# Differential attention: the second softmax's scores leave PSUM by ScalarE, the first softmax's sum moves into the head norm's constant, and three heads share one norm chain

## The chip, the core and the metric

The kernel runs on one core of a Trainium2 chip. The core has a matrix engine (TensorE, PE in the profile; its weight loads are listed apart as PEld), a vector engine (VectorE, DVE), a scalar engine for activations and copies (ScalarE, ACT), a general engine (GpSimd, POOL), and SyncE (SP), which issues most of the DMAs. PE reads SBUF and writes PSUM; DVE and ACT read and write both. Each engine runs its own queue in order, and semaphores tie the queues together. The metric is the device time of one execution in microseconds (us), lower is better; the median of several runs is compared.

## What is computed

One block of a hybrid network over 1024 tokens of width 1024, with 256 tokens of context: a Hyena branch, a differential attention branch, a gated mix of both, and a gated FFN. The change lies in the attention alone. It has 4 heads; each has two softmaxes over 1024+256 keys with 64-wide queries and keys, and one value of 128. Cut to what matters:

```python
def block(qi):                                   # 128 queries of a head
    s = einsum('bhiqd,bhikd->bhiqk', qi, k) * HEAD_DIM ** -0.5     # i = 0, 1
    p = softmax(s, axis=-1)
    a = p[:, :, 0] - lam * p[:, :, 1]
    return einsum('bhqk,bhkv->bhqv', a, v)

def rmsnorm(x, g):
    return x * rsqrt(mean(x * x, axis=-1) + EPS) * g

def heads_out(o, subln_g, lam_init):
    return rmsnorm(o, subln_g) * (1.0 - lam_init)
```

Everything is fp32. A product that needs full precision is made of three matmuls on numbers split into a high and a low half (`hi`, `lo`).

## The kernel before

The program is written as tiles with names; a scheduler orders each engine's queue by its own estimate of when operands and buffers come free, in the main following the order of the code. A tile with a tag shares a ring of buffers with its like, and an allocation waits for the oldest user of the ring.

The attention stage loops over 4 heads (`hd`) and, in each, over 4 groups of 256 queries (`qg`): 16 calls of `attn_group`. `load_head` brings the keys `KS` (one tile for each softmax) and the values `VH`, `VL` from DRAM, and each group loads its queries `Q`. For each of the two blocks of 128 queries (`qt`) and each softmax `i`, PE writes the scores in chunks of 512, 512 and 256 keys into a PSUM bank `S` (tag `S`, 3 banks). Line 808, on DVE, takes each chunk out of PSUM into `pr` (tag `P`, `NP` = 5 buffers of 1280), multiplies it by -1/8 and keeps a running minimum, `prev`, from chunk to chunk. `act(pr, pr, AF.Exp, ...)` then runs on ACT over all 1280 and adds up the softmax's sum into a column of `st_`. DVE takes the reciprocals of both sums (L813) and multiplies the second by `neglam`; ACT scales the second exponentials by it (`AF.Copy` with `scale`); and a `scalar_tensor_tensor` on DVE (helper `stt`, L80) makes the first exponentials times their reciprocal plus the scaled second ones. Calls go through helpers, so rows of the profile often carry the helper's line: `tt` is L77, `stt` L80, `ts` L83, `act` L86.

Then `mid` runs, a list of other work that the group may have in its middle, and the weighted sum follows: PE transposes the probabilities into `pt` (L826), ACT copies them to `ah` (L830) and DVE makes the low half `al` (L77), and PE adds up 30 matmuls into `pv` (L835 to L837). ACT copies `pv` to `ov` and squares it into `osq`, PE sums the squares over partitions (L844) and DVE copies the sums into two columns of `ssall` (L847).

While heads 0 to 2 run, PE fills in with the projections of the next head (`qkv_parts`; L134, operands `h_hi`, `h_lo`). In head 3 it fills in with `hy_up` (L134, operand `z`), the first product of the mix, and with the head norms `y_norm(0)` to `y_norm(2)`. `FILL3` sets which: its entries 10, 11, 12 are `y_norm`, the others `hy_up`. The first entry is `(10, 0)`, `y_norm(0)` and then `hy_up(0)`. Both take a PSUM tile of tag `accb`, two buffers, in the order of the code. `open_mix` frees the projections' operands and loads `z`.

A norm starts with `y_rstd`: 13 small steps on DVE from 8 columns of `ssall` to `rs`, by a bit trick and three Newton steps (`rsqrt_tail`). `y_scale` multiplies the identity by four columns of `rs` on DVE (`dg`, L83), PE broadcasts them by a matmul with ones (L893), and an `stt` scales `yr`. Head 3's own norm follows the loop: `y_rstd(NH - 1, cp)`, then `y_scale` on a PSUM tile `bcp`.

## Time and profile before

| | |
|---|---|
| median of 3 runs | 1852.08 us (1849.85 to 1852.66) |
| profiled execution, its own time | 1849.88 us |
| its span, first to last instruction | 1847.7 us |
| PE busy | 1751.7 us, 95% of the span |
| DVE busy | 1278.9 us, 69% |
| ACT busy | 751.5 us, 41% |
| POOL busy | 58.1 us, 3% |
| TensorE clock granted, mean | 0.979 |
| attention stage (first scores to the last head's sums) | about 632 to 945 us of the span |

The profile lists for each group of instructions its line, its engine, what it writes and reads, its busy time and the idle time of the engine just before it with the instruction that ended it. Matmuls overlap in their pipeline, so that a matmul's duration is longer than the distance to the next; a gap between weight loads tells more of a waiting PE than a gap between matmuls. Shares over the whole span mix stages with different limits, and the questions here are put to the attention stage alone.

### The profile page before, as it was taken

What the parts mean: (1) busy time and instruction counts of PE and PEld (TensorE: products, weight loads), DVE (VectorE), ACT (ScalarE), POOL (GpSimd) and SP (SyncE); (2) the same over time, 40 slices, a digit from 0 to 9 for tenths busy, and PEclk for the clock granted to TensorE, in tenths of its full rate; (3) what the DMA queues carried; (4) which work ended last, traced back from release to release, by engine and by line L of the source; (5) the groups of instructions that cost most, each with busy time, mean ns of one, the idle gap of its engine ahead of it and who ended that gap; (6) DMA issues with size and microseconds to landing.
All of it is one profiled execution on the core that took longest, in us unless ns stands there. A gap on an engine that the chain in (4) does not pass through costs nothing.

```text
span 1847.7 us, 22554 instructions
## 1 busy us (share of the span) xinstructions
PE 1751.7 (95%) x8122; PEld 1408.0 (76%) x8122; DVE 1278.9 (69%) x2277; ACT 751.5 (41%) x1179; POOL 58.1 (3%) x63
## 2 busy tenths in 40 slices
PE   7999989999996999999998899989999999899997
PEld 3588778787875888887876687777778888788886
DVE  5888787776868689898849547967886666323234
ACT  3511323222232466767755257634344343222221
POOL 0000000000000212110100000000000000000000
PEclk9899999999998999999999899989999999999998
DMA  8344533324266834437348743333354225967432
GB/s 331 99 171 175 176 120 131 107 93 154 80 236 230 242 92 137 126 115 233 110 160 285 249 145 119 126 114 114 137 175 156 103 103 178 318 216 210 137 92 68
DMA packets 190111, 293.92 MB, mean 159 GB/s; under 512 B 15235, under 2 KB 110223, under 8 KB 188720
## 3 DMA queue, kind: packets, MB, share of 16 engines
q1 hardware_dynamic: 183776, 284.82, 46.6%
q10 hardware_dynamic: 6224, 7.66, 1.4%
q8 instruction: 64, 1.05, 0.2%
q14 instruction: 47, 0.39, 0.1%
HBM read 213.78 MB, written 78.64 MB: 158 GB/s over the span
## 4 chain that ended last, share of the span: by engine, by line
PE 72%; DVE 18%; DMA 5%; issue 2%; ACT 2%; ACTq 0%; SPq 0%; DVEq 0%
PE pj L1181 20%; PE ps L1043 17%; PE ps L134 16%; DVE pair L77 4%; PE S L804 4%; DVE quad L77 3%; PE pt L826 2%; PE psf L392 2%; PE psf L393 2%; PE psf L537 1%; PE pv L835 1%; PE psf L576 1%; PE psf L378 1%; PE pv L837 1%; DVE wlo L77 1%
## 5 line engine op out<-in xcount | busy, mean ns | idle before, releaser
L77 DVE TENSOR_TENSOR wlo<-wraw,whi 128x1024 fp32r<-128x1024 f32 (+1 forms) x192 | 181.4, 948 | 262.9 <-ACT whi L126 128.5
L126 ACT CAST whi<-wraw 128x1024 fp32r<-128x1024 f32 (+1 forms) x119 | 118.1, 993 | 206.6 <-PE ps L1043 159.0
L134 PE MATMUL ps<-h_hi,wlo 128*128 128x512 f32 x640 | 174.3, 402 | 0.7 <-DVE wlo L77 0.7
L134 PE MATMUL ps<-h_hi,whi 128*128 128x512 f32 x640 | 172.5, 400 | 0.0
L134 PE MATMUL ps<-h_lo,whi 128*128 128x512 f32 x640 | 168.0, 395 | 0.0
L134 PEld LDWEIGHTS ps<-h_hi,wlo 128*128 128x128 f32 x640 | 119.6, 190 | 25.2 <-DVE wlo L77 1.6
L134 PEld LDWEIGHTS ps<-h_lo,whi 128*128 128x128 f32 x640 | 120.0, 189 | 24.4
L134 PEld LDWEIGHTS ps<-h_hi,whi 128*128 128x128 f32 x640 | 119.2, 190 | 22.9
L1181 PE MATMUL pj<-hfc,whi 128*128 128x512 f32 x528 | 131.1, 390 | 0.0
L1181 PEld LDWEIGHTS pj<-hfc,whi 128*128 128x128 f32 x528 | 99.1, 188 | 21.1
L804 PE MATMUL S<-KS,Q 128*128 128x512 f32 (+1 forms) x384 | 107.6, 374 | 3.1 <-DVE pr L808 2.6
L486 ACT COPY gt<-ps 128x512 f32<-128x512 f32 x56 | 32.9, 588 | 188.5 <-PE ps L134 149.0
L1181 PE MATMUL pj<-hfb,whi 128*128 128x512 f32 x352 | 91.7, 404 | 8.7 <-ACT whi L1173 8.6
L1181 PE MATMUL pj<-hfa,whi 128*128 128x512 f32 x352 | 88.9, 393 | 1.4 <-ACT whi L1173 1.3
L1181 PEld LDWEIGHTS pj<-hfb,whi 128*128 128x128 f32 x352 | 67.0, 192 | 27.0 <-ACT whi L1173 11.2
L1173 ACT CAST whi<-s 128x512 fp32r<-128x512 f32 x66 | 40.5, 620 | 100.9 <-DVE s L77 81.8
L1181 PEld LDWEIGHTS pj<-hfa,whi 128*128 128x128 f32 x352 | 65.6, 188 | 16.4 <-ACT whi L1173 2.2
L804 PEld LDWEIGHTS S<-KS,Q 128*128 128x128 f32 x384 | 64.4, 189 | 17.4 <-DVE pr L808 9.4
L1173 ACT CAST whi<-wraw 128x512 fp32r<-128x512 f32 x88 | 53.3, 619 | 56.6 <-PE pj L1181 46.8
L1181 PE MATMUL pj<-hfc,wlo 128*128 128x512 f32 x264 | 70.5, 389 | 0.0
L77 DVE TENSOR_TENSOR quad<-psf,xb 128x512 f32<-128x512 f32 x64 | 41.0, 683 | 35.9 <-ACT xb L250 35.9
L77 DVE TENSOR_TENSOR al<-pt,ah 128x512 fp32r<-128x512 f32 x80 | 52.2, 685 | 10.9 <-ACT ah L830 10.2
(492 smaller groups left out, 3618.2 us busy)
## 6 DMA issues: line engine op xcount, KB each, us to landing
wraw<-win SPq DMA_DIRECT2D x46, 512.0 KB, 3.7
wraw<-wdown SPq DMA_DIRECT2D x88, 256.0 KB, 3.3
wada_t<-wada SPq DMA_DIRECT2D x32, 512.0 KB, 7.5
wraw<-wgate SPq DMA_DIRECT2D x28, 512.0 KB, 3.3
wraw<-wupf SPq DMA_DIRECT2D x28, 512.0 KB, 3.7
ad<-kp SPq DMA_DIRECT2D x44, 256.0 KB, 2.1
w_ada<-wada SPq DMA_DIRECT2D x16, 512.0 KB, 6.6
kspec<-quad SPq DMA_DIRECT2D x8, 1024.0 KB, 3.9
```

What stands on the lines that cost most here:

```text
L77: (eng or V).tensor_tensor(out=out, in0=a, in1=b, op=op)
L126: A.copy(out=hi, in_=raw)
L134: T.matmul(out=ps, lhsT=w[:, k * P:(k + 1) * P], rhs=xs[k][j], start=start and i == 0, stop=stop and i == len(seq) - 1)
L378: T.matmul(out=ps, lhsT=a[:, cs], rhs=b, start=i == 0, stop=i == 2)
L392: T.matmul(out=out, lhsT=mfm(part, r), rhs=gen[r][:, 0:256], start=True, stop=False)
L393: T.matmul(out=out, lhsT=mfm(pb, rb), rhs=gen[rb][:, 256:512], start=False, stop=True)
L486: A.copy(out=gt, in_=ps)
L804: T.matmul(out=S[:, :cn], lhsT=Q[j][:, i, qt * P:(qt + 1) * P], rhs=KS[i][:, c0:c0 + cn], start=j == 0, stop=j == 1)
L826: T.transpose(out=pt[:, b * 256 + qt * P:b * 256 + (qt + 1) * P], in_=av[qt][:, kt * P:(kt + 1) * P], identity=ident)
L1043: T.matmul(out=acc[b].rearrange("p (m c) -> p m c", m=4), lhsT=xs[kk][i == 1][:, b * P:(b + 1) * P], rhs=w[i == 2][kk], start=first and (k ...
L1173: A.copy(out=hi, in_=src)
L1181: T.matmul(out=ps, lhsT=w[a][:, k * P:(k + 1) * P], rhs=xs[k][b], start=i == 0, stop=i == 11)
```

## The change

Four things change, all in the attention stage.

1. The probabilities are no longer divided by the first softmax's sum s0. The exponentials are combined as P0 + (-lam s0 / s1) P1, which is s0 times what it was. The head norm that follows is made of sums of squares, so that a factor s0 cancels if its constant EPS is multiplied by s0 squared. The sums s0 are kept in a new tile `s0all`, one column for each 128 queries. ACT's scaling pass over the second exponentials goes away.
2. The second softmax's three score chunks leave PSUM by `A.copy` on ACT; one DVE instruction over all 1280 elements, in place in SBUF, then multiplies by -1/8 and finds the minimum. The first softmax's chunks stay as they were.
3. `y_rstd` is called once for heads 0 to 2, inside `y_norm(0)`, on 24 columns, with two more steps (the square of `s0all`, and its product with EPS), and once for head 3.
4. `y_scale` makes `dg` on ACT.

```diff
+    s0all = ap.tile([P, 32], F32, name="s0all")
...
             st_ = a2.tile([P, 12], F32, tag="st", bufs=4, name="st_")
+            c0_ = hd * 8 + qg * 2 + qt
+            sums = [s0all[:, c0_:c0_ + 1], st_[:, 3:4]]
...
+                    if i == 1:
+                        A.copy(out=pr[:, c0:c0 + cn], in_=S[:, :cn])
+                        continue
 
                     mc = st_[:, 6 + 3 * i + c:7 + 3 * i + c]
                     V.tensor_scalar(out=pr[:, c0:c0 + cn], in0=S[:, :cn], scalar1=-0.125, scalar2=prev,
                                     op0=ALU.mult, op1=ALU.min, accum_out=mc)
                     prev = mc
-                act(pr, pr, AF.Exp, bias=prev, scale=-1.0, accum_out=st_[:, 2 + i:3 + i])
+                if i == 1:
+                    prev = st_[:, 9:10]
+                    V.tensor_scalar(out=pr, in0=pr, scalar1=-0.125, scalar2=None, op0=ALU.mult, op1=ALU.min,
+                                    accum_out=prev)
+                act(pr, pr, AF.Exp, bias=prev, scale=-1.0, accum_out=sums[i])
                 pp.append(pr)
-            V.reciprocal(out=st_[:, 4:6], in_=st_[:, 2:4])
-            tt(st_[:, 5:6], st_[:, 5:6], neglam, ALU.mult)
-            act(pp[1], pp[1], AF.Copy, scale=st_[:, 5:6])
-            stt(pp[0], pp[0], st_[:, 4:5], pp[1], ALU.mult, ALU.add)
+
+            V.reciprocal(out=st_[:, 4:5], in_=sums[1])
+            stt(st_[:, 5:6], sums[0], neglam, st_[:, 4:5], ALU.mult, ALU.mult)
+            stt(pp[0], pp[1], st_[:, 5:6], pp[0], ALU.mult, ALU.add)
...
-    def y_rstd(hd, pool_):
-        cs = slice(hd * 8, hd * 8 + 8)
-        w = pool_.tile([P, 24], F32, tag="yrs", bufs=2, name="yrs")
-        ts(w[:, 0:8], ssall[:, cs], 1.0 / P, EPS, ALU.mult, ALU.add)
-        rsqrt_tail(w[:, 8:16], w[:, 0:8], w[:, 16:24])
-        ts(rs[:, cs], w[:, 8:16], 1.0 - LAM_INIT, None, ALU.mult, ALU.bypass)
+    def y_rstd(h0, h1, pool_):
+
+        cs, n = slice(h0 * 8, h1 * 8), (h1 - h0) * 8
+        w = pool_.tile([P, 72], F32, tag="yrs", bufs=1, name="yrs")
+        m, r, q = [w[:, i * 24:i * 24 + n] for i in range(3)]
+        tt(r, s0all[:, cs], s0all[:, cs], ALU.mult)
+        ts(m, ssall[:, cs], 1.0 / P, None, ALU.mult, ALU.bypass)
+        stt(m, r, EPS, m, ALU.mult, ALU.add)
+        rsqrt_tail(r, m, q)
+        ts(rs[:, cs], r, 1.0 - LAM_INIT, None, ALU.mult, ALU.bypass)
...
-            ts(dg[:, b * P:(b + 1) * P], ident, rs[:, c0:c0 + 1], None, ALU.mult, ALU.bypass)
+            act(dg[:, b * P:(b + 1) * P], ident, AF.Copy, scale=rs[:, c0:c0 + 1])
...
     def y_norm(hd):
-        y_rstd(hd, a2)
+        if hd == 0:
+            y_rstd(0, NH - 1, a2)
...
-    y_rstd(NH - 1, cp)
+    y_rstd(NH - 1, NH, cp)
```

The scheduler puts the stage's queues into another order with this. Three places follow; the line numbers of the changed kernel are some 3 to 14 higher than those of the old one (L808 is L814 there, L826 is L836, L893 is L907; L810 is the new copy on ACT, L819 the new pass on DVE).

DVE in the second head, one block of 128 queries, before: six chunks leave PSUM, with `al` of the group before between them, and the two tiny steps and the `stt` follow.

```order
L808 TENSOR_SCALAR pr,st__6063<-S,st__6063 128x256
L808 TENSOR_SCALAR pr,st__6096<-S 128x512
L808 TENSOR_SCALAR pr,st__6096<-S,st__6096 128x512
L813 RECIPROCAL st__6063<-st__6063 128x2
L808 TENSOR_SCALAR pr,st__6096<-S,st__6096 128x256
L77 TENSOR_TENSOR al<-pt,ah 128x512 x2
L77 TENSOR_TENSOR st__6063<-st__6063,lamc 128x1
L808 TENSOR_SCALAR pr,st__6096<-S 128x512
L80 SCALAR_TENSOR_TENSOR pr<-pr,st__6063 128x1280
```

The same place now:

```order
L819 TENSOR_SCALAR pr,st__6064<-pr 128x1280
L814 TENSOR_SCALAR pr,st__6097<-S 128x512
L814 TENSOR_SCALAR pr,st__6097<-S,st__6097 128x512
L814 TENSOR_SCALAR pr,st__6097<-S,st__6097 128x256
L824 RECIPROCAL st__6064<-st__6064 128x1
L80 SCALAR_TENSOR_TENSOR st__6064<-s0all,lamc,st__6064 128x1
L80 SCALAR_TENSOR_TENSOR pr<-pr,st__6064 128x1280
L814 TENSOR_SCALAR pr,st__6230<-S 128x512
L819 TENSOR_SCALAR pr,st__6097<-pr 128x1280
```

Three chunks of each pair are replaced by one pass over `pr`, which stands between chunks of other blocks.

ACT in the first head, third group, before: exponentials (two names of `st_` each) and scalings (`pr<-pr,st`), with `ah` between them.

```order
L86 ACTIVATE pr,st__4982<-pr,st__4982 128x1280
L86 ACTIVATE pr,st__5187<-pr,st__5187 128x1280
L86 ACTIVATE pr<-pr,st__4982 128x1280
L86 ACTIVATE pr,st__5187<-pr,st__5187 128x1280
L830 CAST ah<-pt 128x512 x2
L86 ACTIVATE pr<-pr,st__5187 128x1280
```

The same place now:

```order
L810 COPY pr<-S 128x512
L840 CAST ah<-pt 128x512 x2
L86 ACTIVATE pr,s0all<-pr,st__5188 128x1280
L810 COPY pr<-S 128x256
L840 CAST ah<-pt 128x512 x2
L86 ACTIVATE pr,st__5188<-pr,st__5188 128x1280
L86 ACTIVATE pr,s0all<-pr,st__5221 128x1280
```

The scalings are gone, and copies out of `S` stand behind exponentials and `ah` on the same queue.

PE where the first `hy_up` matmul stands (operand `z`), before: in the weighted sum of a group, soon after the projections of the heads have run out.

```order
L837 MATMUL pv<-al,VH 128x256
L826 MATMUL pt<-ident,pr 128x128 x8
L804 MATMUL S<-KS,Q 128x256 x2
L134 MATMUL ps<-z_7114,whi 128x512
L835 MATMUL pv<-ah,VH 128x256
L836 MATMUL pv<-ah,VL 128x256
L134 MATMUL ps<-z_7115,whi 128x512
```

The same place now, where `ps<-dg,ones` are the broadcasts of `y_norm(0)`:

```order
L807 MATMUL S<-KS,Q 128x256 x2
L807 MATMUL S<-KS,Q 128x512 x4
L907 MATMUL ps<-dg,ones 128x512
L836 MATMUL pt<-ident,pr 128x128 x2
L807 MATMUL S<-KS,Q 128x256
L907 MATMUL ps<-dg,ones 128x512
L134 MATMUL ps<-z_7115,whi 128x512
L134 MATMUL ps<-z_7116,whi 128x512
```

`hy_up` now follows the second broadcast directly and runs in a row. Between the last projection matmul and the first `hy_up` matmul stand 136 matmuls before and 213 now.

## Rows read from the trace of the kernel before

**Rows 1.** The page's busy times: engine, busy us, share of the span, instructions.

```profile
PE 1751.7 (95%) x8122; PEld 1408.0 (76%) x8122; DVE 1278.9 (69%) x2277; ACT 751.5 (41%) x1179; POOL 58.1 (3%) x63
```

**Rows 2.** Windows: us; PE, PEld, DVE, ACT, POOL busy (instructions); clock, DMA share, GB/s.

```profile
632.00:945.00 313.00, 307.42 (x1772) 253.81 (x1772) 272.80 (x705) 213.54 (x325) 39.66 (x23) 1.00 0.41 132
842.00:867.00 25.00, 23.10 (x132) 16.83 (x131) 23.18 (x68) 17.81 (x28) 0.82 (x1) 1.00 0.89 303
867.00:945.00 78.00, 77.83 (x453) 64.47 (x454) 62.67 (x160) 53.99 (x89) 6.54 (x4) 1.00 0.32 104
```

**Rows 3.** Waits of weight loads, 632 to 945 us: total us, times, longest.

```profile
PEld S L804 <- DVE pr L808: 9.4, 22, 1.3
PEld pv L835 <- ACT ah L830: 8.5, 27, 1.0
PEld pv L844 <- ACT osq L86: 3.9, 12, 0.4
PEld pt L826 <- DVE pr L80: 3.1, 5, 1.2
PEld pv L837 <- DVE al L77: 3.1, 11, 0.6
```

**Rows 4.** Waits of PE's weight loads, 842 to 867 us.

```profile
PEld S L804 <- DVE pr L808: 3.5, 9, 0.8
...
PEld pt L826 <- DVE pr L80: 1.2, 1, 1.2
...
PEld pv L837 <- DVE al L77: 0.9, 2, 0.6
```

**Rows 5.** Timeline, 856 to 862 us: start, us, engine, instruction, idle before.

```profile
856.19 4.55 PE L804 MATMUL S<-KS,Q 128*128 128x256 f32 x14
...
861.70 0.63 PEld L826 LDWEIGHTS pt<-ident,pr 128*128 128x128 f32 x6 [1.17 <-DVE pr L80]
```

**Rows 6.** Timeline, 635 to 644 us: evictions and `stt` on DVE, weight loads.

```profile
635.31 0.69 DVE L808 TENSOR_SCALAR_CACHE_REDUCE pr<-S 128x512 f32<-128x512 f32 x1
...
635.92 0.48 DVE L808 TENSOR_SCALAR_CACHE_REDUCE pr<-S,st__4477 128x256 f32<-128x256 f32 x1
...
636.33 0.75 DVE L808 TENSOR_SCALAR_CACHE_REDUCE pr<-S,st__4477 128x512 f32<-128x512 f32 x1
...
637.00 0.08 DVE L808 DVE_READ_ACCUMULATOR pr<-S,st__4477 128x1 f32 x1
...
643.64 1.58 PEld L134 LDWEIGHTS ps<-h_hi,whi 128*128 128x128 f32 x7
643.68 1.54 DVE L80 SCALAR_TENSOR_TENSOR pr<-pr,st__4477 128x1280 f32<-128x1280 f32 x1
```

**Rows 7.** Lines by form, whole span: busy us, mean ns of one, idle before.

```profile
L753 ACT CAST c_hi<-cx 128x256 fp32r<-128x256 f32 x8 | 2.8, 406 | 11.3 <-DVE cx L83 11.3
...
L83 DVE TENSOR_SCALAR sy<-sy 128x512 f32<-128x512 f32 x6 | 2.6, 426 | 0.2
```

**Rows 8.** Timeline, ACT: a scaling pass, copies out of PSUM.

```profile
642.14 1.37 ACT L86 ACTIVATE pr<-pr,st__4477 128x1280 f32<-128x1280 f32 x1 [0.20 <-DVE st__4477 L77]
...
697.25 0.37 ACT L839 COPY ov<-pv 128x256 f32<-128x256 f32 x1 [1.41 <-PE pv L837]
...
706.19 1.04 ACT L830 CAST ah<-pt 128x512 fp32r<-128x512 f32 x2
```

**Rows 9.** Timeline, 945 to 950 us, the last head's norm.

```profile
945.67 0.17 DVE L83 TENSOR_SCALAR yrs<-ssall 128x8 f32<-128x8 f32 x1
...
948.38 1.66 DVE L83 TENSOR_SCALAR dg<-ident,rs 128x128 f32<-128x128 f32 x8
949.33 0.30 PEld L893 LDWEIGHTS bcp<-dg,ones 128*128 128x128 f32 x2 [1.99 <-ACT whi L126]
```

**Rows 10.** Timeline, 705 us, POOL and DVE side by side.

```profile
705.00 2.40 POOL L77 TENSOR_TENSOR wlo<-wraw,whi 128x1024 fp32r<-128x1024 f32 x1 [26.30 <-ACT whi L126]
...
705.33 2.62 DVE L77 TENSOR_TENSOR t<-t,sw 128x512 f32<-128x512 f32 x1
```

## The prediction

> **What bounds the kernel now.** I read the page's busy times first, then the stage by windows, then who waits for whom on PE. Over the whole span PE is busy 1751.7 us (95%) and DVE 1278.9 [rows 1]. The change touches the attention stage, from the first score matmul at 632 us to the last head's sums at 945. There DVE is busy 272.80 of 313.00 us (87%), ACT 213.54 (68%), and PE counts as busy for 307.42, while its weight loads fill 253.81 [rows 2]. A busy PE hides gaps, since the modelled ends of matmuls overlap, so I go by the waits of the weight loads: 9.4 us (22 times) for DVE to take a score bank out of PSUM, 3.1 us (5 times) for the combined probabilities, 3.1 us (11 times) for the low half `al`; against ACT 8.5 us (27 times) for `ah` and 3.9 us (12 times) for the squares [rows 3]. That is 28 us, about 15.6 of them DVE's. Some 0.04 us of each is the ordinary gap between two loads (seven of 0.19 in 1.58 us, rows 6), so perhaps 25 us of the 313 can be won at the very most. The granted clock is 1.00 in each of these windows [rows 2], so it is no part of the sum.
>
> The loss is uneven. From 842 to 867 us the weight loads fill 16.83 of 25 us (67%), from 867 to 945 64.47 of 78 (83%) [rows 2], and 5.6 of DVE's 15.6 us fall into those 25 us [rows 4]. There PE has no projection to fill in with. Seven pairs of score matmuls are spread over 4.55 us, and then the transposes wait 1.17 us for the `stt` on DVE [rows 5]. I call it the bare stretch.
>
> **Evictions.** For each 128 queries the second softmax now loses three DVE instructions that read PSUM. Counted from start to start, since neighbours overlap, they take 0.61, 0.41 and 0.67 us [rows 6], 1.69 together, with the accumulator reads inside. It gains one DVE pass over 128x1280 in SBUF with the same minimum, which the trace does not show. From above: the `stt` over 1280 takes 1.54 with the overlap [rows 6], so about 1.45 without. From below: the same 512 elements take 0.426 us from SBUF in a plain multiply and add, against 0.69 from PSUM with the minimum [rows 6, 7], and the slope of rows 6, 0.26 us for 256 elements, gives 0.61+0.78=1.39 at the slow rate and about 0.87 at the fast one. I take 1.39, as the row of the same operation is the nearest, and keep 0.87 to 1.45. Times 32: 9.6 us of DVE work less (7.7 to 26).
>
> The Trainium skill, in "VectorE: DVE Perf Modes", section "The perf-mode tier table", gives a plain fp32 `tensor_scalar` in SBUF twice the rate of one that reads PSUM; by it the pass would cost about 0.8 us, an estimate from its 1227 ns for 2048 elements. The plain multiply of rows 7 agrees with that; no row shows a pass that also keeps a minimum.
>
> ACT gains three copies out of PSUM, by the rows of like size 1.04 for the two wide ones and 0.37 for the 256 wide, and loses the scaling of 1280 elements, 1.37 [rows 8]: 1.41 against 1.37, so nothing. The path from the last score bank to the finished probabilities keeps its length too. Before: a DVE eviction, an exponential, two tiny steps, the ACT scaling, the `stt`. After: an ACT copy, the DVE pass, an exponential, two tiny steps, the `stt`. The reciprocal and the step after it stay two tiny DVE steps.
>
> **Norms.** Three chains of 13 DVE steps become one of 15. A chain alone runs from 945.67 to 948.38, 0.208 a step [rows 9], so 24 steps are 5.0 us. The 24 `dg` steps of heads 0 to 2 leave DVE at 0.207 each (eight in 1.66, rows 9): 5.0 us. On ACT they cost less than the 0.41 of a 256-wide instruction [rows 7], so under 10 us, in a stage in which ACT is idle for 99. The last head's chain is two steps longer (0.4 us), and its eight `dg` stand on ACT too; they lie before a broadcast for which PE already waits 1.99 us [rows 9], so I give this 0, at most +1.
>
> **DVE's sum**: 9.6+5.0+5.0 = 19.6 us of 272.8, which leaves 253 (81%). One thing can eat into it: an addition of two SBUF tiles over 512 elements took 2.62 us while POOL ran 2.40 beside it [rows 10]. The new pass reads SBUF, its forerunners PSUM. POOL is busy 13% of the stage [rows 2]; if the pass suffers the same way, 32 x 0.13 x about 1 us gives 4 us back. I leave that in the range.
>
> **What of it reaches the end.** Outside the bare stretch, PE waits for DVE's evictions 9.4-3.5=5.9 us, for the `stt` 1.9 and for `al` 2.2 [rows 3, 4]; less 0.04 us for each of the 26, 9 us. DVE's idle time grows from 40 to 60 us, so its busy-to-idle ratio falls from 6.8 to 4.2, and I let the waits fall in that proportion (0.62). Of the score banks only half still wait for DVE. So 5.5 x (1-0.31) = 3.8 us go on the scores and 3.5 x 0.38 = 1.3 on the others: -5.1. Against it, scores now wait for ACT, behind exponentials as long as the scaling pass, 1.37 us, on its queue [rows 8]; `ah`, five to a group and 80 in all, costs PE 8.5 us [rows 3], and the 96 new ones have three banks of slack, so +0.5 (0 to +3). With the norms' work out of head 3, -1.5 (0 to -3). The waits for `ah` and for the squares I leave as they are, since ACT's load hardly changes.
>
> The bare stretch grows. In the order before, 136 matmuls lie between the last projection of the heads and the first `hy_up` matmul, now 213: `y_norm(0)` stands ahead of `hy_up(0)` and takes its PSUM tile first, and its constant now needs head 2's sums. The stretch loses (0.83-0.67) x 25 = 4 us now; at 213/136 it would lose 6.3, and 6% less DVE work takes a little off. So +2 (0 to +8; the upper end is three times today's loss, as if DVE alone set the pace there).
>
> On SP the loads of `Q` and of weights change places by a few issues; no PE wait of the stage ends on a DMA [rows 3], so 0. Sum: -5.1+0.5-1.5+2 = -4.1, with ends at -13 and +8. The profiled execution took 1849.88 us (span 1847.7), so 1845.8; the median of the three runs lies 2.2 higher, at 1852.08, so **1848.0** on that scale. The FFN behind it is shifted unchanged.
>
> **Rivals.** *The relief goes deeper* (0.14): the SBUF pass runs at the fast rate, 32 x 0.52 = 16.6 us more off DVE. At the rate of the sum above, 5.1 us for 19.6, that is 4 to 5 more: 1843. For it speaks the plain multiply of rows 7, against it that this one has a minimum to keep. By the rule of the Trainium skill cited above it would come out like this.
> *The relief stays in DVE's idle time* (0.31): DVE is in order, and the new pass waits for the third ACT copy, itself queued behind exponentials; the waits change their name but not their length. 1850 to 1854, no difference that can be seen. For it speaks that the path keeps its length, and that this also happens if the pass costs 1.45 plus POOL's share, when DVE sheds too little.
> *The merged norm starves PE* (0.23), the slower side: `hy_up` is held behind a constant that needs three heads, and the longer stretch runs at DVE's pace. From +6 in the stretch on it outweighs the gains elsewhere: +8 with -4 there, 1856. For it: the 213 matmuls and the 67% of rows 2. Against it: the projections that are not used there fill PE later and are not lost.
>
> **Chances and range.** The forecast itself, 2 to 8 us faster than the median, 0.32. A measurement of this kernel can tell about 0.2%, 3.7 us. Faster by more than that: most of the forecast and the deeper case, 0.45; within: 0.31; slower: 0.24. The range 1837 to 1858 leaves out the ends of both tails; the forecast's own range is 1844 to 1850.
>
> **What would show it.** Right: DVE busy near 253 us in the stage, ACT within 8 of 214, weight loads waiting for evictions under 6 us in total, PE's bare stretch longer but not emptier. A pass over 1280 near 0.8 us means the deeper case. Wrong: a total of PE waits as large as before with ACT's name on the score banks, or over 8 us of waits between the last projection and the first `hy_up` matmul.

## The result, and the profile after

The changed kernel is slower: 1864.62 us median (1862.02 to 1870.7, 6 runs) against 1852.37 for the kernel before, measured beside it (1849.85 to 1854.43, 6 runs). The ratio of the runs is 1.0077, with a 95% interval of 1.0065 to 1.0089; the two medians alone give 1.0066. The prediction was 1848.0 and its range ended at 1858. The profiled span grew from 1847.7 to 1862.4 us.

The attention stage now runs from 632 to 965 us of the span. Its busy times (us; PE, PEld, DVE, ACT, POOL with instructions; clock, DMA share, GB/s), to be read against [rows 2]:

```profile
632.00:965.00 333.00, 317.49 (x1775) 253.88 (x1774) 257.82 (x530) 222.91 (x413) 40.84 (x22) 0.99 0.40 124
```

DVE did shed the work: 272.8 us became 257.8, in a stage that is 20 us longer. But the waits of the weight loads did not shrink with it. They answer to [rows 3]; the columns are the total in us, how often, and the longest:

```profile
PEld pv L845 <- ACT ah L840: 13.4, 42, 0.8
PEld pv L847 <- DVE al L77: 9.4, 19, 2.1
PEld S L807 <- DVE pr L814: 9.1, 22, 1.2
PEld pt L836 <- issue: 6.0, 11, 3.0
PEld pt L836 <- DVE pr L80: 5.8, 9, 1.0
PEld S L807 <- ACT pr L810: 3.7, 12, 0.8
PEld pv L854 <- ACT osq L86: 2.0, 6, 0.6
```

The waits for `ah` grew from 8.5 to 13.4 us, for `al` from 3.1 to 9.4, for the combined probabilities from 3.1 to 5.8. DVE's score banks are half as many and still cost 9.1 us. The 3.0 us put down to "issue" are a weight load just ahead of a matmul that itself waits for the `stt`, as a timeline below shows.

**Where the time went.** For each matmul I took the distance to the next one, less the lower quartile for its form, as lost time, and added it up in three parts: from the first scores to the last projection matmul, from there to the first product of the mix (the bare stretch), and on to the last head's sums.

| | to the last projection | bare stretch (its length) | to the stage's end | stage | behind it to the last matmul |
|---|---|---|---|---|---|
| before | 13.4 | 6.8 (26.7 us) | 6.0 | 313.8 us | 74.9 lost in 898.1 |
| after | 24.1 | 16.2 (48.1 us) | 3.7 | 333.2 us | 69.8 lost in 893.3 |

So the stage is 19.4 us longer: 10.7 are lost among the projections, 9.4 in the bare stretch, 2.3 come back behind it, and 1.6 this measure doesn't place. The stages that follow give another 4.8 us back. Two losses have to be explained, each about 10 us.

### The profile page after: what moved, and what is told of

It reads as the page before. It is cut to its first block, busy times and chain, and to the rows that moved or that the text cites. A ratio compares the mean times of both kernels' runs of the same rounds, so it can differ in the third digit from the quotient of the medians.

```text
span 1862.4 us, 22438 instructions
## 1 busy us (share of the span) xinstructions
PE 1755.4 (94%) x8122; PEld 1404.6 (75%) x8122; DVE 1262.6 (68%) x2095; ACT 762.8 (41%) x1275; POOL 59.8 (3%) x63
## 3 DMA queue, kind: packets, MB, share of 16 engines
q8 instruction: 64, 1.05, 0.2%
## 4 chain that ended last, share of the span: by engine, by line
PE 65%; DVE 19%; DMA 7%; ACT 4%; issue 3%; SPq 0%; POOL 0%; ACTq 0%; DVEq 0%
PE pj L1196 19%; PE ps L1058 16%; PE ps L134 13%; DVE pair L77 4%; DVE quad L77 3%; PE S L807 3%; PE psf L392 2%; PE psf L393 2%; PE pt L836 1%; PE psf L537 1%; DVE pr L80 1%; PE psf L576 1%; PE psf L378 1%; PE pv L845 1%; DVE wlo L77 1%
## 5 line engine op out<-in xcount | busy, mean ns | idle before, releaser
L134 PEld LDWEIGHTS ps<-h_lo,whi 128*128 128x128 f32 x640 | 119.9, 189 | 24.3
L807 PEld LDWEIGHTS S<-KS,Q 128*128 128x128 f32 x384 | 63.5, 193 | 19.9 <-DVE pr L814 9.1
```

The source lines that it names most:

```text
L134: T.matmul(out=ps, lhsT=w[:, k * P:(k + 1) * P], rhs=xs[k][j], start=start and i == 0, stop=stop and i == len(seq) - 1)
L807: T.matmul(out=S[:, :cn], lhsT=Q[j][:, i, qt * P:(qt + 1) * P], rhs=KS[i][:, c0:c0 + cn], start=j == 0, stop=j == 1)
```

## The experiments

Twenty kernels are compared below; each was timed against the kernel before on its own chip, so the ratio counts and not the median. An interval is some 0.001 to 0.0025 to either side. The columns on the right are read from one profiled execution of each kernel: the loss as above, when its first scores start, how long the stage is from there to the last head's sums, and how long it is from these to the last matmul.

| kernel | ratio (95%) | lost to the last projection | lost in the bare stretch (its length) | first scores at | stage | behind it |
|---|---|---|---|---|---|---|
| before | 1 | 13.4 | 6.8 (26.7) | 631.6 | 313.8 | 898.1 |
| changed kernel | 1.0077 (1.0065 to 1.0089) | 24.1 | 16.2 (48.1) | 631.6 | 333.2 | 893.3 |
| e1: changed, a chain per head | 1.0085 (1.0059 to 1.0110) | 24.3 | 11.2 (30.7) | 634.6 | 329.4 | 892.0 |
| e2: before + merged chain | 1.0047 (1.0030 to 1.0064) | 11.3 | 16.9 (51.5) | 632.6 | 323.5 | 895.9 |
| e3: before + ACT evictions and pass | 1.0105 (1.0087 to 1.0124) | 19.8 | 11.5 (32.4) | 635.8 | 329.5 | 899.3 |
| e4: before + s0 in the constant | 1.0040 (1.0027 to 1.0052) | 17.8 | 13.5 (30.9) | 633.7 | 325.6 | 895.8 |
| e5: changed, `hy_up(0)` first | 1.0063 (1.0048 to 1.0078) | 24.0 | 1.0 (5.4) | 631.2 | 330.2 | 891.8 |
| e6: changed, DVE evictions | 0.9990 (0.9974 to 1.0006) | 16.0 | 17.0 (45.1) | 636.6 | 322.0 | 889.4 |
| e7: e6 with a chain per head | 1.0008 (0.9992 to 1.0024) | 18.3 | 12.2 (33.2) | 628.8 | 323.6 | 891.3 |
| e8: changed, six buffers | 1.0090 (1.0072 to 1.0109) | 25.6 | 18.5 (51.5) | 632.6 | 337.4 | 889.2 |
| e9: before + `dg` on ACT | 1.0016 (1.0003 to 1.0030) | 14.6 | 9.1 (28.6) | 635.4 | 318.4 | 895.7 |
| e10: changed, no DVE pass | 1.0036 (1.0018 to 1.0055) | 17.8 | 14.5 (46.8) | 633.2 | 322.3 | 895.9 |
| e11: before + two more DVE passes | 1.0028 (1.0012 to 1.0044) | 13.4 | 7.8 (27.8) | 635.7 | 318.2 | 900.7 |
| e14: changed, exponentials from PSUM | 1.0019 (1.0006 to 1.0032) | 23.2 | 12.8 (35.4) | 632.9 | 325.6 | 890.8 |
| f1: changed, POOL's work on DVE | 1.0029 (1.0016 to 1.0042) | 18.9 | 21.2 (41.6) | 624.7 | 332.3 | 892.3 |
| f3: e14, POOL's work on DVE | 0.9988 (0.9979 to 0.9998) | 17.4 | 13.9 (37.3) | 627.8 | 321.1 | 894.2 |
| f4: e6, POOL's work on DVE | 0.9987 (0.9974 to 0.9999) | 14.6 | 16.1 (49.2) | 626.0 | 320.9 | 897.9 |
| f5: before, POOL's work on DVE | 0.9995 (0.9984 to 1.0006) | 15.3 | 8.4 (24.3) | 625.7 | 320.5 | 897.6 |
| g1: f4 with a chain per head | 0.9949 (0.9929 to 0.9969) | 15.0 | 6.5 (28.9) | 626.6 | 315.0 | 897.0 |
| g2: f3 with a chain per head | 0.9978 (0.9962 to 0.9993) | 15.3 | 10.9 (29.5) | 632.6 | 317.9 | 892.1 |

How far can one execution be trusted? The kernel before and e11 have the same order on every engine up to 870 us. Their first scores start 4.1 us apart, and from there to 857 us that distance stays within 0.1 us. So a stretch of the stage repeats well, but the time ahead of it does not: the fourteen kernels with the same 2621 matmuls in the same order ahead of the first scores reach them at 628.8 to 636.6 us. Some of these executions (e3, e6, e11) are also 4 to 5 us above the median of their kernel. So I compare stages to the microsecond, and what lies ahead and behind only roughly.

### The merged chain and the evictions, one at a time (e1, e2, e3, e5)

e1, a chain per head in the changed kernel:

```diff
-        if hd == 0:
-            y_rstd(0, NH - 1, a2)
+        y_rstd(hd, hd + 1, a2)
```

> The changed kernel with one change taken back: each head's norm chain runs alone on its 8 columns, as before, so that y_norm(0) needs head 0 alone. The order then has 127 matmuls between the last projection and the first hy_up matmul, not 213. Theory N (the merged chain holds hy_up back and starves PE): the changed kernel loses about 16 us of PE's time between 850 and 890 us where the old one loses about 6, so 8 to 10 of its 12 us come back: 1853 to 1856. Theory E (the evictions on ACT are the cause, through a longer ping-pong of ACT and DVE in every group): the stretch matters little, 1861 to 1864.

e2, the merged chain alone on the kernel before:

```diff
-        y_rstd(hd, a2)
+        if hd == 0:
+            y_rstd(0, NH - 1, a2)
```

> The kernel before with one change alone: the norm chain of heads 0 to 2 in one call inside y_norm(0). Evictions, scaling and dg stay on their engines. The order has 235 matmuls in the bare stretch, before 136. Theory N: slower than before by 6 to 12 us, 1858 to 1864, and all of it between the last projection and the first hy_up matmul. Theory E: within 3 us of before, or a little faster, since DVE loses 26 small steps.

e3, the evictions alone on the kernel before (ACT's scaling pass stays):

```diff
+                    if i == 1:
+                        A.copy(out=pr[:, c0:c0 + cn], in_=S[:, :cn])
+                        continue
...
+                if i == 1:
+                    prev = st_[:, 9:10]
+                    V.tensor_scalar(out=pr, in0=pr, scalar1=-0.125, scalar2=None, op0=ALU.mult, op1=ALU.min,
+                                    accum_out=prev)
```

> The kernel before with one change alone: the second softmax's chunks leave PSUM by ACT and one DVE pass finds the minimum; the scaling on ACT stays, so ACT gains three copies per 128 queries. The bare stretch in the order is 138 matmuls, as before (136). Theory N: within 4 us of before. Theory E: slower by 5 to 12 us, with PE waiting for al, ah and the transposes in the projections' part, 632 to 840 us.

e5, the changed kernel with `hy_up(0)` ahead of `y_norm(0)`, so that products of the mix may run before the constant is there:

```diff
-FILL3 = ((10, 0), (1, 11), (2, 12), (3, 4, 5))
+FILL3 = ((0, 10), (1, 11), (2, 12), (3, 4, 5))
```

> The changed kernel with one entry of FILL3 turned round: hy_up(0) ahead of y_norm(0), so that the fill-in product takes its PSUM tile first. The bare stretch in the order falls to 36 matmuls. Theory N: the loss of 16 us between 850 and 890 shrinks to what the landing of z leaves, 4 to 8 us, so 1852 to 1857. Theory E: 1860 to 1864.

Alone, the merging costs 0.47%, and its loss lies in the bare stretch, which doubles (26.7 to 51.5 us) and loses 16.9 us instead of 6.8, while the projections' part is no worse than before. The evictions alone cost 1.05%, as much as the whole change or more, in both parts. But the prices don't add up: without the merging the changed kernel is not measurably faster (1.0085, with 0.0025 to either side; its stage is 3.8 us shorter), and with `hy_up` first it gets back 0.14%, which the intervals leave open: the stretch shrinks to 5.4 us, but the 16 us that it lost are lost behind it instead (20.1 us from there to the stage's end).

### What the relief of DVE is worth (e4, e6, e7, e9)

e4 takes the changed kernel's `s0all` and `y_rstd`, with DVE's evictions, a chain per head and `dg` on DVE. e9 is the kernel before with one line of the change:

```diff
-            ts(dg[:, b * P:(b + 1) * P], ident, rs[:, c0:c0 + 1], None, ALU.mult, ALU.bypass)
+            act(dg[:, b * P:(b + 1) * P], ident, AF.Copy, scale=rs[:, c0:c0 + 1])
```

e6 is the changed kernel without the evictions on ACT:

```diff
-                    if i == 1:
-                        A.copy(out=pr[:, c0:c0 + cn], in_=S[:, :cn])
-                        continue
...
-                if i == 1:
-                    prev = st_[:, 9:10]
-                    V.tensor_scalar(out=pr, in0=pr, scalar1=-0.125, scalar2=None, op0=ALU.mult, op1=ALU.min,
-                                    accum_out=prev)
```

and e7 is e6 with e1's edit on top.

> Before, with the first sum moved into the norm's constant alone: the scaling pass on ACT goes (32 x 1.37 us), the evictions stay on DVE, dg stays on DVE, one chain per head. Theory E (what costs is the second softmax leaving PSUM by ACT, with the minimum in a pass behind it): nothing of the loss is here; the path from the last score bank to the probabilities is 1.4 us shorter, so 0 to 8 us faster than before, ratio 0.996 to 1.000. Theory O (any edit of this block puts the projections in lumps, and the lumps cost): projections' part 5 or more us slower, ratio 1.003 or more. Theory N (the merged chain alone costs): like E.

> The changed kernel with the second softmax's scores taken out by DVE again (tensor_scalar with the running minimum, three to a bank row), the rest as changed: s0 in the constant, merged chain, dg on ACT. Theory E: the projections' part (632 to 832) goes back to the loss of before, 1.3 to 2 us in 20; the stretch behind the projections still loses about 9 us more than before by the merged chain; the tail gives 4 to 5 back: ratio 0.998 to 1.004. Theory N: everything stays as in the changed kernel, 1.006 to 1.009. Theory O: projections' part still about 9 us slower, 1.005 or more.

> The changed kernel without ACT evictions and without the merged chain: s0 in the constant and dg on ACT remain. Theory E: neither loss is here, so ratio 0.993 to 0.999 (faster by 2 to 12 us, of which 4 to 5 in the stages behind the attention, if they go with dg on ACT). Theory O: 1.003 or more, lost in the projections' part. Against e6 it gives the price of the merging when the evictions are DVE's: about 9 us if the prices are additive, as they were not in e1.

> Before, with the dg steps alone on ACT (0.40 us each, eight to a head). If the 4.7 us that the changed kernel gets back behind the last head's sums belong to dg on ACT: the stretch from the last sums to the end is 897 to 899 us instead of 902, ratio 0.996 to 0.999. If they belong to the other edits: 902 us, ratio 0.999 to 1.001. Theory O: stage longer by 5 us or more.

The comparison of e6 with the changed kernel is the largest in the set: 0.9990 against 1.0077, for the evictions alone; the stage is 11.2 us shorter, and the loss among the projections falls from 24.1 to 16.0 us. That is Theory E, that the evictions on ACT, with the pass behind them, are what costs. Its second half fell: e4 takes 38 us of the stage's work off ACT and is 0.4% slower, with a stage 11.8 us longer; e9 takes 4 us off DVE, puts 7 on ACT, and is no faster. Theory O asked for a ratio like e4's (1.003 or more), while e6 and e7 went against it.

e7 missed as well. Theory E gave it 0.993 to 0.999 and it came to 1.0008, so that against e6 the merging costs nothing even where DVE evicts. From e4 to e7 little changes but that `dg` goes to ACT (`yrs` also has one buffer instead of two): that is worth 0.32%, while on the kernel before the same step costs 0.16%. So an edit's price hangs on the order that the scheduler makes of all of them, and a difference of 0.3% does not by itself show the mechanism that an edit was made for. Each of the four edits alone lengthens the stage of the kernel before, the merging by 9.7 us, the evictions by 15.7, the first sum by 11.8 and `dg` by 4.6: 42 us, where all four together cost 19.4. No run tunes the order anew for the changed kernel, so how much of a price belongs to an edit and how much to its order stays open.

The 4.8 us that the stages behind the attention give back are not `dg`'s either: with it alone 2.4 us of them show (895.7 us behind the last sums, against 898.1), and e11, whose edit lies in the stage, differs by as much the other way (900.7). What they belong to stays open.

### Buffers, the pass, and the bare stretch's edge (e8, e10, e11, e14)

e8 sets `NP = 6`. e10 drops the pass; the second exponential runs without a maximum:

```diff
-                if i == 1:
-                    prev = st_[:, 9:10]
-                    V.tensor_scalar(out=pr, in0=pr, scalar1=-0.125, ...)
-                act(pr, pr, AF.Exp, bias=prev, scale=-1.0, accum_out=sums[i])
+                if i == 1:
+                    act(pr, pr, AF.Exp, scale=0.125, accum_out=sums[i])
+                else:
+                    act(pr, pr, AF.Exp, bias=prev, scale=-1.0, accum_out=sums[i])
```

e14 has ACT take the exponentials straight out of the banks, without copies:

```diff
                     if i == 1:
-                        A.copy(out=pr[:, c0:c0 + cn], in_=S[:, :cn])
+                        act(pr[:, c0:c0 + cn], S[:, :cn], AF.Exp, scale=0.125, accum_out=st_[:, 9 + c:10 + c])
                         continue
...
                 if i == 1:
-                    prev = st_[:, 9:10]
-                    V.tensor_scalar(out=pr, in0=pr, scalar1=-0.125, ...)
-                act(pr, pr, AF.Exp, bias=prev, scale=-1.0, accum_out=sums[i])
+                    tt(st_[:, 9:10], st_[:, 9:10], st_[:, 10:11], ALU.add)
+                    tt(sums[1], st_[:, 9:10], st_[:, 11:12], ALU.add)
+                else:
+                    act(pr, pr, AF.Exp, bias=prev, scale=-1.0, accum_out=sums[i])
```

e11 is the kernel before with a delay that was meant for the bare stretch:

```diff
+            if hd == NH - 1 and qg == 0 and qt == 1:
+                for _ in range(2):
+                    ts(pp[0], pp[0], 1.0, None, ALU.mult, ALU.bypass)
             stt(pp[0], pp[0], st_[:, 4:5], pp[1], ALU.mult, ALU.add)
```

> The changed kernel with six buffers of probabilities instead of five. Ring theory (a second softmax's tile is now taken at its first copy and held through copies, pass, exponential and combination, so that the ring of five runs out and the next scores have nowhere to go): the loss of the projections' part falls from about 24 us to 16 or less, ratio 1.000 to 1.004. Hop theory (the chain from the last score bank over copy, pass, exponential to the combination is what is late, and more buffers don't shorten it): ratio 1.006 to 1.009 as in the changed kernel.

> The changed kernel without the pass over 1280 elements on DVE: the second softmax's scores leave by ACT as changed, and its exponential runs with scale 1/8 and no maximum taken off (that part of the computation is left out). Hop theory: with the pass both the hop to DVE and 45 us of DVE work are gone, the combination is no longer late, the projections' part loses 16 us or less, ratio 0.990 to 0.999. Bank theory (the loss is in score banks that wait for ACT behind 1.4 us exponentials): the waits of weight loads for ACT's copies remain or grow beyond 4 us and the ratio stays above 1.003.

> The kernel before with two more passes of DVE over 1280 elements (times one) ahead of the combination of head 3's first group, in the stretch without projections; nothing else is changed. Edge theory (the stretch of before runs just above where the granted clock falls, and any longer wait there drops it): granted clock 0.5 for 6 us or more after that wait, and the stretch longer by more than the added DVE time allows, 5 to 7 us in all: ratio 1.0025 to 1.004. Without an edge: clock 1.00, and at most the two passes' own 2 x 1.4 us or less: ratio 0.9995 to 1.0015.

> The changed kernel with the second softmax's exponentials taken by ACT directly out of the three score banks, scale 1/8, no maximum taken off (that part is left out), their three sums added in two tiny DVE steps: no copy, no pass, no exponential over 1280. Against the changed kernel DVE loses 45 us more and ACT 44 us. Hop theory: no hop at all is left and the combination comes early: ratio 0.985 to 0.997. Bank theory: ACT still holds the banks, behind the first softmax's exponential: ratio 1.000 or more.

More buffers change nothing, so the ring theory is out. e10 and e14 are the telling ones. Each does without the pass (32 x 1.41 = 45 us of DVE's work), e14 without ACT's exponentials over 1280 too (its pieces take the place of the copies), and still both are slower than the kernel before. e14's weight loads:

```profile
PEld pv L845 <- ACT ah L840: 11.8, 39, 0.8
PEld S L807 <- DVE pr L814: 8.5, 16, 2.2
PEld pv L847 <- DVE al L77: 7.3, 16, 2.1
PEld S L807 <- ACT pr L86: 5.7, 16, 1.2
```

From its first scores to its last sums, e14's weight loads wait 19.9 us for DVE and 22.7 for ACT, against 15.6 and 12.4 in the kernel before, although between 632 and 950 us DVE is busy 71% instead of 87% and ACT 58% instead of 68%. The other runs agree. DVE's busy share of the stage and the waits put down to it are 87% and 15.6 us before, 77% and 25.3 in the changed kernel, 67% and 19.2 in e10, 82% and 18.4 in f1, 89% and 9.9 in g1. So an engine's load alone doesn't set these waits, which the prediction's sum took for granted. Nor does the path from the scores: from the end of a block's last score matmul to the end of its `stt` I read 10.6 us on average over the 32 blocks before, 8.1 after, 8.5 in e6.

Without the pass (e10) the loss among the projections falls by 6.3 us and the stage by 10.9, nearly as much as without the evictions (e6, 11.2). That points to the pass, its work or its place on the path, and not to the copies on ACT; but the order changes with it. The hop theory asked for more: a loss of 16 us or less, and a ratio under 1. The marks of the bank theory came in (4.2 us of waits for ACT's copies and 1.0036 in e10, 1.0019 in e14), but 4.2 and 5.7 us of waits for ACT's banks are a small part of the loss.

e11 doesn't test the edge. The `stt` that its two passes stand ahead of comes late in the order, and they ran behind the bare stretch, which ends at 871.8 us there:

```profile
877.36 0.82 DVE L83 TENSOR_SCALAR pr<-pr 128x1280 f32<-128x1280 f32 x1
...
879.33 0.82 DVE L83 TENSOR_SCALAR pr<-pr 128x1280 f32<-128x1280 f32 x1
```

The granted clock nevertheless falls in the stretch, where it was 1.00 before (windows of 2 us, columns as above):

```profile
858.00:860.00 2.00, 1.59 (x8) 0.78 (x7) 1.60 (x5) 0.11 (x1) 0.00 (x0) 1.00 1.04 287
860.00:862.00 2.00, 1.88 (x7) 1.06 (x7) 1.88 (x8) 1.46 (x2) 0.00 (x0) 0.74 0.85 301
862.00:864.00 2.00, 2.00 (x7) 1.24 (x6) 1.90 (x8) 1.03 (x1) 0.00 (x0) 0.50 0.86 283
864.00:866.00 2.00, 1.23 (x6) 0.87 (x4) 2.00 (x5) 2.00 (x4) 0.00 (x0) 0.90 0.93 329
```

Until then every engine runs the instructions of the kernel before, in its order and at its distances. The seven pairs of score matmuls that took 4.55 us at a clock of 1.00 in [rows 5] are these:

```profile
860.28 4.95 PE L804 MATMUL S<-KS,Q 128*128 128x256 f32 x14
```

So in this stretch the clock fell in one execution and not in another, with nothing changed ahead of it, and a fall in a single profile can't by itself be put down to an edit. It lasted 3.4 us, where the edge theory asked for 6 or more, and cost these matmuls 0.4 us. The stretch is 1.1 us longer instead of 5 to 7, and the rest of the 4.4 us by which the stage grows comes behind it, where the passes ran; so the ratio, which lies in the theory's range, is no support for it. A fall of the clock alone doesn't tell what a stretch loses: e14 loses 12.8 us in its bare stretch with the clock at 1.00 throughout, g1 6.5 us with a fall in it.

### The collision of DVE and POOL (f1, f3, f4, f5)

In the changed kernel PE's two longest waits among the projections are for `al`, 2.12 us at 718.42 and 1.70 at 745.55. Here is the first, as the timelines of DVE, POOL and the weight loads have it (start, us, engine, instruction, idle before and what ended it):

```profile
714.36 0.68 DVE L77 TENSOR_TENSOR t<-ps,rp 128x512 f32<-128x512 f32 x1
714.95 2.81 DVE L77 TENSOR_TENSOR sw<-sw,rp 128x512 f32<-128x512 f32 x1
717.69 0.68 DVE L77 TENSOR_TENSOR al<-pt,ah 128x512 fp32r<-128x512 f32 x1
```

```profile
714.84 2.37 POOL L77 TENSOR_TENSOR wlo<-wraw,whi 128x1024 fp32r<-128x1024 f32 x1 [2.20 <-ACT whi L126]
```

```profile
718.42 0.19 PEld L847 LDWEIGHTS pv<-al,VH 128*128 128x128 f32 x1 [2.12 <-DVE al L77]
```

`sw` times `rp` is a product of the rotary embedding. It has two operands in SBUF and takes 0.68 us by itself; here it starts 0.11 us after POOL's low half of a weight and ends 0.55 us after that. `al` stands behind it on DVE, PE behind `al`. The row of 705 us [rows 10] is the same collision in the kernel before, where an eviction stood right behind it: of the 54 `al` steps up to 850 us three directly follow a rotary product there, and begin 1.9 us in all after the end of their `ah`; in the changed kernel it is nine of 52, and 11.8 us. The Trainium skill, "SBUF — State Buffer", section "Who interferes with whom", states that a DVE instruction with two SBUF inputs contends with a GpSimd instruction that reads SBUF; the rows agree. The same section excepts the `tensor_scalar` that writes out its accumulator from those that can contend, and the pass agrees: all 32 took 1.47 to 1.49 us, three of them while POOL ran.

So the low halves of weights, queries and keys go from POOL to DVE, in four kernels:

```diff
-    RENG, RLENG = V, G
+    RENG, RLENG = V, V
...
-    LO[0] = G
```

> The changed kernel with the low halves of weights, queries and keys made by DVE instead of POOL in the attention stage. Pool theory (PE's waits for al come from rotary products that POOL's work stretches from 0.7 to 2.8 us): the products all take about 0.69, the weight loads' waits for al fall from 9.4 us to 3 or less, the projections' part loses 18 us or less instead of 24, DVE's busy time in the stage rises by about 20 us, ratio 1.001 to 1.005. Order theory (the scheduler's order leaves PE alone with the round trips, whoever is slow in them): waits for al or ah stay above 18 us together, ratio 1.006 or more.

> The kernel with the second softmax's exponentials straight from PSUM (no maximum taken off, that part is left out), and POOL's low halves made by DVE. DVE has 45 us less to do than in the changed kernel and gets 20 back. Pool theory: the loss of the projections' part falls from 22 us to 16 or less, ratio 0.993 to 0.999. Order theory: ratio 1.001 or more.

> The changed kernel with DVE's evictions, and POOL's low halves made by DVE: DVE's busy time in the stage near that of the kernel before again or above it. Pool theory: the products are short again, but waits for al were small (0.4 us) with DVE's evictions, so little to win, and 20 us more DVE work to pay: ratio 1.000 to 1.005. Order theory: anything between 0.997 and 1.005.

> The kernel before, with POOL's low halves made by DVE: DVE, 87% busy in the stage, gets about 20 us more (and some 5 back from products that are no longer stretched). If DVE's load bounds the stage of before: ratio 1.004 to 1.010. If DVE's load doesn't bound it, as the runs with less of it suggest (45 us less did not make it faster): ratio 0.999 to 1.003.

f1 gains 0.48% on the changed kernel, about 9 us. The groups of DVE's rotary products up to 850 us, in f1 (busy us, mean ns of one, idle before):

```profile
L77 DVE TENSOR_TENSOR sw<-sw,rp 128x512 f32<-128x512 f32 x9 | 6.2, 685 | 0.0
```

and in the changed kernel:

```profile
L77 DVE TENSOR_TENSOR sw<-sw,rp 128x512 f32<-128x512 f32 x10 | 12.0, 1198 | 0.0
```

The products are short, f1's waits for `al` fall from 9.4 to 3.0 us, and the loss among the projections from 24.1 to 18.9, all close to what the Pool theory asked for (f3's loss, 17.4 us, stays above its 16). But that is not where the 0.48% comes from. The bare stretch loses 5.0 us more (21.2), and the stage is as long as the changed kernel's (332.3 us against 333.2). Of the 8.8 us by which f1's profile is ahead at the last matmul, 6.9 are there at the first scores. The edit acts there too: between 500 us and the first scores POOL is busy 15.3 us in the changed kernel and not at all in f1. Here are five pairs that differ by POOL's work alone (the last three columns in us, from the table above):

| with POOL's work on DVE | ratio | first scores | stage | behind it |
|---|---|---|---|---|
| f1 less the changed kernel | -0.0048 | -6.9 | -0.9 | -1.0 |
| f3 less e14 | -0.0031 | -5.1 | -4.5 | +3.4 |
| f4 less e6 | -0.0003 | -10.6 | -1.1 | +8.5 |
| f5 less before | -0.0005 | -5.9 | +6.7 | -0.5 |
| g1 less e7 | -0.0059 | -2.2 | -8.6 | +5.7 |

The first scores come earlier in all five, by 6 us on average, while the stage gains up to 8.6 us or loses 6.7. Where ACT evicts it gains 0.9 and 4.5 us; the largest gain, g1's, is one with DVE's evictions. So the collision is shown as the reason of the long waits for `al`, but not as the reason of a loss in the stage, and a longer stage elsewhere takes back what the waits give. Nor does it explain a part of what the evictions cost. By the ratios they cost 0.87% with POOL's work on POOL (the changed kernel against e6) and 0.42% with it on DVE (f1 against f4), but the stage is 11.2 and 11.4 us longer with them; the ratios differ by what lies ahead of the stage and behind it. In e3 only three `al` follow a rotary product, and its stage is 15.7 us longer than that of the kernel before. Beside the pass, the table of waits names `ah` and the banks on ACT (f1: 12.2 and 6.1 us, e6: 10.2 and none), which no run here takes apart.

### A version faster than both (g1, g2)

g1 and g2 are f4 and f3 with e1's edit.

> f4 (DVE's evictions, the first sum in the constant, dg on ACT, POOL's low halves on DVE) with one norm chain per head. If the merging costs the 9 us that it cost alone on the kernel before (e2): the stretch from the last projection to the first product of the mix falls from 49 to about 33 us, and the ratio from 0.9987 to 0.994 or 0.995. If it costs nothing beside the other edits, as with the changed kernel (e1): 0.998 to 1.000.

> f3 (the second softmax's exponentials straight from PSUM without a maximum, which is left out; POOL's low halves on DVE) with one norm chain per head. Merging dear: ratio 0.994 or 0.995. Merging free: 0.998 to 1.000.

g1 is faster than the kernel before by 0.51% (0.31 to 0.71; its five runs' median, 1844.52 against 1851.20 us, gives 0.36%), and than the changed one by 1.3%. Against f4 the merging costs 0.38% there, with the stretch 49.2 us long instead of 28.9 and 16.1 us lost in it instead of 6.5. That is e2's price in e2's place, though with POOL at work (e6 against e7) it was nothing. g2 gains 0.1% on f3, which is within what the intervals leave open. In the profile g1's gain is not in the stage, which is 315.0 us long against 313.8: its first scores come 5.0 us earlier. g1's stage:

```profile
632.00:945.00 313.00, 306.65 (x1767) 254.81 (x1765) 277.88 (x718) 182.15 (x318) 0.00 (x0) 0.99 0.42 131
```

DVE is busier than in [rows 2], 277.9 against 272.8 us, PE gets through as much, and what is gone is ACT's scaling pass and all of POOL's work.

## Why the prediction was wrong

**What held.** The working of DVE's load: 253 us were forecast and 257.8 came. The pass:

```profile
L819 DVE TENSOR_SCALAR_CACHE_REDUCE pr<-pr 128x1280 f32<-128x1280 f32 x32 | 47.4, 1482 | 5.6 <-ACT pr L810 5.3
```

From start to start it is 1.41 us, where 1.39 was taken. The rival that had it at the fast rate is out. The rule of the Trainium skill that the prediction cited for it ("VectorE: DVE Perf Modes", "The perf-mode tier table"; 0.8 us by it, an estimate) is for a plain `tensor_scalar`. For that e11 agrees, whose two plain passes took 0.82 us each, but it doesn't hold for one that also keeps a minimum. `dg` on ACT took 0.40 us where under 0.41 was said. The path from the last bank didn't lengthen. Scores waiting for ACT cost 3.7 us, a little past the upper end of "+0.5 (0 to +3)".

**The step that failed first** is "what of it reaches the end": -5.1 us, from the rule that PE's waits for an engine fall with that engine's busy-to-idle ratio. DVE's waits should have fallen by a third or more; they rose from 15.6 to 24.3 us (9.4, 9.1 and 5.8), not counting those put down to issue. Put down to DVE in all there were 15.6 us before and 25.3 after, and DVE's load does not set them: f1 has 13 us more DVE work in its stage than the changed kernel and waits 18.4 us, e10 has 42 less and waits 19.2. Of the 10.7 us that came among the projections in place of the relief, 8.1 go when DVE evicts again (e6) and 6.3 when only the pass is left out (e10); the prediction had the evictions there as a gain. Each of these waits is for one instruction at one place in an in-order queue, and what stands ahead of it there is decided by the order. The change altered the order everywhere, and the prediction priced only the work. That the order is the whole reason is argued, not shown.

**"The waits for `ah` and for the squares I leave as they are, since ACT's load hardly changes"** failed in the same way: 8.5 us became 13.4, though ACT's load, 222.9 us, was 9 above the 214 of which it was to stay within 8. The waits for the squares fell, from 3.9 to 2.0.

**The bare stretch** was sized by its matmuls, 4 us lost x 213/136, so +2. The mechanism and the place were right, as e2 shows on its own, but the size was +9.4, just above the upper end of +8. The stretch has a poorer mix than the old one: it takes in the end of the last group with its `stt`. From the changed kernel's PE and DVE timelines:

```profile
868.60 0.66 PE L836 MATMUL pt<-ident,pr 128*128 128x128 f32 x2 [2.80 <-DVE pr L80]
868.91 2.48 PE L807 MATMUL S<-KS,Q 128*128 128x512 f32 x6
871.87 2.41 PE L807 MATMUL S<-KS,Q 128*128 128x512 f32 x6 [0.48 <-ACT pr L810]
```

```profile
865.36 0.75 DVE L814 TENSOR_SCALAR_CACHE_REDUCE pr<-S,st__7137 128x512 f32<-128x512 f32 x1
...
866.04 0.16 DVE L824 RECIPROCAL st__6940<-st__6940 128x1 f32<-128x1 f32 x1
866.24 0.48 DVE L814 TENSOR_SCALAR_CACHE_REDUCE pr<-S,st__7137 128x256 f32<-128x256 f32 x1
...
866.65 0.21 DVE L80 SCALAR_TENSOR_TENSOR st__6940<-s0all,lamc,st__6940 128x1 f32<-128x1 f32 x1
...
866.90 1.55 DVE L80 SCALAR_TENSOR_TENSOR pr<-pr,st__6940 128x1280 f32<-128x1280 f32 x1
```

The transposes wait 2.80 us for an `stt` that is late in its turn: its exponential's sum was read at 865.00 to 865.19, but on DVE the reciprocal stands behind one eviction and the next small step behind another, all in order. Then the clock is at half (windows of 2 us):

```profile
866.00:868.00 2.00, 0.00 (x0) 0.00 (x0) 1.95 (x8) 2.00 (x4) 0.00 (x0) 0.80 0.87 299
868.00:870.00 2.00, 1.40 (x5) 1.24 (x6) 1.85 (x3) 0.33 (x3) 0.00 (x0) 0.50 1.01 407
870.00:872.00 2.00, 1.52 (x6) 1.03 (x4) 0.56 (x3) 2.00 (x4) 0.00 (x0) 0.50 1.04 412
872.00:874.00 2.00, 2.00 (x6) 1.61 (x6) 2.00 (x2) 0.58 (x2) 0.00 (x0) 0.50 1.01 397
```

A score matmul then takes 0.43 us from start to start instead of 0.23, and there are about a dozen, so some 2 us of the 9.4 are the clock's, an estimate from these two distances.

**The norms** were to give 1.5 us. e9, e1 and e2 find no such gain.

**The range** sets the ends -13 and +8 on the profiled execution's 1849.88 us, the forecast on the median, 2.2 us higher. On one scale it would run from 1839 to 1860, and the result lies above either.

**The rivals.** "The merged norm starves PE" (0.23) named one of the two losses and its place: it put +8 into the stretch, which lost 9.4 us more, and 10.1 more in e2. It counted on 4 us of gain elsewhere that weren't there. No rival had the evictions themselves as a loss; the nearest, "the relief stays in DVE's idle time", comes closest in its reason, an in-order DVE, but let the waits change only their name. The sentence that the FFN behind would be "shifted unchanged" failed too, by 4.8 us in the change's favour in these two profiles. In the kernel before PE waits in the 75 us behind the stage 4.1 us for `wlo` on DVE, 2.8 for `whi` and 1.6 at the last norm's broadcast. Now these two are left, 1.1 us less in all:

```profile
PE ps L134 <- ACT whi L126: 5.2, 2, 4.7
PE bcp L907 <- ACT dg L86: 2.2, 1, 2.2
```

## What to carry to other kernels

Taking work off an engine that is 87% busy was worth nothing here, where PE's waits are for single instructions in in-order queues; ask of each waiting instruction what will stand ahead of it in the new order, since that can change with any edit. Price edits one at a time and together, because the sums don't add: the merging cost 0.47% alone, nothing beside ACT's evictions or in e6, and 0.38% in f4. See where in the span a gain lies before you put it down to the mechanism that an edit was made for: f1's waits did what was forecast, and its gain lay ahead of the stage. See also that an added delay ran where it was meant to. And look at what a second engine does at that moment before an engine's own load is blamed.

## What the runs showed of the hardware

POOL's help was worth little to DVE here. With POOL's low halves on DVE (f5) the whole span has these busy times, to be read against [rows 1]:

```profile
PE 1756.0 (95%) x8122; PEld 1411.2 (76%) x8122; DVE 1286.7 (70%) x2308; ACT 751.8 (41%) x1179; POOL 3.4 (0%) x32
```

POOL is rid of 54.7 us. DVE took over 31 instructions of 26.1 us and is 7.8 us busier; the rest it got back from products that were no longer stretched to as much as 2.9 us.

A `tensor_scalar` over 128x1280 from SBUF to SBUF takes 0.82 us when it only multiplies (e11), and 1.48 us when it also keeps a minimum (L819 in the changed kernel).

The granted clock of the bare stretch is not settled by the queue order alone. From 852 to 872 us the kernel before has

```profile
852.00:872.00 20.00, 18.10 (x99) 12.81 (x99) 18.61 (x51) 13.09 (x22) 0.00 (x0) 1.00 0.80 260
```

and e11, with the same instructions there up to 870 us, falls to 0.50 for 3.4 us. Most of the profiles have a fall to 0.50 in that stretch, for 3.4 to 17 us in all; the kernel before, e5 (a stretch of 5.4 us), e14 and f5 have none.
